# Attention with V as the held operand: two heads in the two halves of the array's columns, and probabilities divided ahead of their transposes

## The chip, the core and the metric

The kernel runs on one core of one Trainium2 chip. A core has five engines that run side by side, each with an instruction queue of its own: TensorE (PE in the profile; its weight loads are PEld), VectorE (DVE), ScalarE (ACT), GpSimd (POOL) and SyncE (SP, which here issues the loads from memory). The metric is the device time of one execution in microseconds (us); lower is better.

## The reference

A two-layer decoder trunk on 256 tokens of 1024 features, in float32. Layer 0 mixes tokens with a gated recurrence, layer 1 with attention; each layer has a SwiGLU feed-forward block of width 2816 before and after its mixer. The change lies in the attention of layer 1 (16 heads of 64, causal, with a forget gate whose running sum `c` is added to the logits):

```python
for blk in range(S // Q_BLOCK):            # two blocks of 128 queries
    q0 = blk * Q_BLOCK
    end = q0 + Q_BLOCK
    logits = jnp.einsum('bhqd,bhkd->bhqk', q[:, :, q0:end], k[:, :, :end]).astype(jnp.float32)
    logits = logits + c[:, :, q0:end, None] - c[:, :, None, :end]
    logits = jnp.where(kpos[None, :] <= qpos[:, None], logits, -jnp.inf)
    p = jax.nn.softmax(logits, axis=-1).astype(v.dtype)
    outs.append(jnp.einsum('bhqk,bhkd->bhqd', p, v[:, :, :end]))
o = jnp.concatenate(outs, axis=2).transpose(0, 2, 1, 3).reshape(Bn, S, D_ATTN)
return o @ w_o
```

## The kernel before

The 256 tokens are two tiles of 128 (t = 0 and 1). Every large product is made of three matmuls in a fast float32 form: operands are split into an upper and a lower part (`hi`, `lo`), and `mm3` (L183) adds hi x hi, hi x lo and lo x hi into one PSUM bank. Weights stream in from memory in tiles of 128 x 1024 (`load_raw`, issued by SP into five buffers) and are split by `split` (L165): ScalarE copies the upper part (L174), VectorE subtracts to get the lower part (L179). For the output projection `w_o` (`row_items` with `dve=True`) every second tile is split the other way: VectorE copies the upper part (L172), GpSimd subtracts (also L179).

TensorE's order is the program's own: it runs what the code issues, in that order. The other engines' orders are set by a scheduler when the program is built, with work inside `tc.high_priority()` put first; once built, each engine's order is fixed and each engine works through its queue strictly in turn.

In the attention stage the string `ATT_ORDER` (L1105) is TensorE's order: `0` and `1` are weight blocks of the projections for token tile 0 or 1 (first the query projection, sixteen entries in all, then the output projection), `a0` and `a1` are attention steps of a tile. A step works on head groups, of four heads for tile 0 (`per` = 4, one key tile) and of two heads for tile 1 (`per` = 2, two key tiles). Step i issues up to four things: the logits of group i (`logits`), the products with V of group i-3 (`values`), the transposes of the probabilities of group i-2 (`turn`), and, after every eighth head, the transposes of the output (`output`). Within `logits`, VectorE adds the mask (L1031) and takes the negative row maximum (L1033), and ScalarE takes the exponentials of each head into `pe` with the row sum as a side result in `sm` (L1038). `turn` makes four transposes of 128 x 128 into a PSUM bank (L1046), and ScalarE copies them to `pT` (L1048). `values` holds the transposed probabilities in the array and moves 64 columns of V (L1057), with the queries on the partitions of the result `po`; when eight heads are done, VectorE inverts the row sums (L1060) and multiplies (L1062) into `ot`. `output` transposes `ot` back to features on partitions (L1069), and writes its upper part on ScalarE (`oh`, L1072) and its lower part on VectorE (`ol`, L1073) as operands of the output projection.

While tile 0 is attended, the query projection of tile 1 (block by block) and its head transposes (`heads_T`, L921, L926, L929, L930) run between the steps.

Of the kernel before, what the change touches and what calls it, by code (L numbers as in the profile page):

```python
# [9 lines left out]
F32 = mybir.dt.float32  # L10
F32R = mybir.dt.float32r
BF16 = mybir.dt.bfloat16
AF = mybir.ActivationFunctionType
ALU = mybir.AluOpType
AX = mybir.AxisListType

P = 128
# [8 lines left out]
HD = 64  # L26
# [18 lines left out]
def trunk_kernel(ctx: ExitStack, tc: tile.TileContext, A: dict, out: bass.AP):  # L45
    nc = tc.nc
# [11 lines left out]
    def nm(s):  # L58
        uid[0] += 1
        return f"{s}_{uid[0]}"  # L60

    def mmbank():
        return psum.tile([P, 512], F32, tag="mm", name=nm("mm"), bufs=4)

    def gtbank():
        return psum.tile([P, 512], F32, tag="gt", name=nm("gt"), bufs=2)

    def trbank():
        return psum.tile([P, 512], F32, tag="tr", name=nm("tr"), bufs=2)
# [44 lines left out]
    ident = cpool.tile([P, P], F32, name="ident")  # L114
# [760 lines left out]
    kv = {}  # L875
# [133 lines left out]
    att = {}  # L1009
# [7 lines left out]
    def attention(t):  # L1017

        ap = pools["a"]
        nk = t + 1  # L1020
        per = 4 // nk
        mask = kv["cmask"].unsqueeze(1).to_broadcast([P, per, P])
        box = {}
        G = NH // per

        def logits(hg):
            hds = range(hg * per, (hg + 1) * per)
            ps = gtbank().rearrange("p (a b) -> p a b", a=per)
            for j, hd in enumerate(hds):
                nc.tensor.matmul(ps[:, j, :], att["q"][t][:, hd, :], kv["kT"][:, hd, :nk * P], start=True, stop=True)  # L1030
            nc.vector.tensor_tensor(ps[:, :, t * P:], ps[:, :, t * P:], mask, ALU.add)  # L1031
            mx = spool.tile([P, 4], F32, tag="mx", name=nm("mx"))
            nc.vector.tensor_reduce(mx[:, :per], ps, AX.X, ALU.max, negate=True)  # L1033
            if hds[0] % 8 == 0:
                box["sm"] = spool.tile([P, 8], F32, tag="sm", name=nm("sm"))
            pe = ap.tile([P, per, nk * P], F32, tag="pe", name=nm("pe"), bufs=3)
            for j, hd in enumerate(hds):
                nc.scalar.activation(pe[:, j, :], ps[:, j, :], AF.Exp, bias=mx[:, j:j + 1],  # L1038
                                     accum_out=box["sm"][:, hd % 8:hd % 8 + 1])
            box["pe", hg], box["s", hg] = pe, box["sm"]  # L1040

        def turn(hg):
            tp = trbank()
            pev = box["pe", hg].rearrange("p a b -> p (a b)")
            for j in range(4):
                nc.tensor.transpose(tp[:, j * P:(j + 1) * P], pev[:, j * P:(j + 1) * P], ident)  # L1046
            pT = box["pT", hg] = ap.tile([P, 4, P], F32, tag="pT", name=nm("pT"), bufs=3)
            nc.scalar.activation(pT.rearrange("p a b -> p (a b)"), tp, AF.Copy)  # L1048

        def values(hg):  # L1050
            hds = range(hg * per, (hg + 1) * per)
            if hds[0] % 8 == 0:
                box["po"] = mmbank()
            po, pT, sm = box["po"], box["pT", hg], box["s", hg]
            for j, hd in enumerate(hds):
                for k in range(nk):
                    nc.tensor.matmul(po[:, (hd % 8) * HD:(hd % 8 + 1) * HD], pT[:, j * nk + k, :],  # L1057
                                     kv["v"][k][:, hd * HD:(hd + 1) * HD], start=k == 0, stop=k == nk - 1)
            if hds[-1] % 8 == 7:
                nc.vector.reciprocal(sm, sm)  # L1060
                ot = box["ot", hds[-1] // 8] = ap.tile([P, 8, HD], F32, tag="ot", name=nm("ot"), bufs=2)
                nc.vector.tensor_tensor(ot, po.rearrange("p (a b) -> p a b", a=8),  # L1062
                                        sm.unsqueeze(2).to_broadcast([P, 8, HD]), ALU.mult)

        def output(b):
            otv = box["ot", b].rearrange("p a b -> p (a b)")
            tp = trbank()
            for j in range(4):
                nc.tensor.transpose(tp[:, j * P:(j + 1) * P], otv[:, j * P:(j + 1) * P], ident)  # L1069
            oh_v = att["oh"][t][:, 4 * b:4 * b + 4, :].rearrange("p a b -> p (a b)")  # L1070
            ol_v = att["ol"][t][:, 4 * b:4 * b + 4, :].rearrange("p a b -> p (a b)")
            nc.scalar.activation(oh_v, tp, AF.Copy)  # L1072
            nc.vector.tensor_tensor(ol_v, tp, oh_v.bitcast(F32), ALU.subtract)  # L1073

        steps = []
        for i in range(G + 4):
            s = []
            if i < G:
                s.append(lambda i=i: logits(i))
            if 0 <= i - 3 < G:  # L1080
                s.append(lambda i=i: values(i - 3))
            if 0 <= i - 2 < G:
                s.append(lambda i=i: turn(i - 2))
            j = i - 4
            if j >= 0 and (j + 1) * per % 8 == 0:
                s.append(lambda j=j: output((j + 1) * per // 8 - 1))
            steps.append(s)
        return steps

# [3 lines left out]
    for n in range(2):  # L1093
# [8 lines left out]
    ffn_items(lambda: pools["f"], A["ffn2_w_gate"][1], A["ffn2_w_up"][1], A["ffn2_w_down"][1], A["ffn2_post_g"][1],  # L1102
              lambda t: None, last=True)

    ATT_ORDER = ("0 0 0 0 0 0 0 0 a0 1 a0 1 1 1 a0 1 a0 1 a0 1 a0 a1 1 a0 "  # L1105
                 "0 a1 a0 a1 0 a1 0 a1 0 a1 0 a1 0 a1 0 a1 0 a1 1 a1 1 a1 1 1 1 1 1 1")


    def half(t, i):
# [161 lines left out]
    defer(6, att_rows)  # L1271

    steps = [attention(0), attention(1)]
    nxt = [n_ffn3, n_ffn3]
    for c in ATT_ORDER.split():
        if c[0] == "a":
# [46 lines left out]
```

## Time and profile before

| | |
|---|---|
| median of 3 runs | 1000.72 us (1000.6 to 1001.02) |
| the profiled execution | 1001.29 us |
| its span, first to last instruction | 999.3 us |
| granted TensorE clock, mean | 0.998 |
| attention stage | about 743 to 798 us of the span |

Row names in the views: a line number of the kernel, the engine, the operation, the tile written and the tiles read. In the list of groups the columns are count, total busy time and mean ns of one. In the view of stages each engine has its busy time and, in brackets, its instruction count, in the order PE, PEld, DVE, ACT, POOL; then come the granted clock, the DMA engines' share and GB/s. In the chain in order of time a row has the start, what the step added to the chain, and the step. In the timeline a row has the start and the duration of an instruction (or of a few of one kind, x4), and in square brackets how long its engine was idle before and what ended that. Matmuls overlap in the pipeline, so what a matmul costs is the step to the next one, not its own duration.

### The profile page before, as it was taken

How to read it: one execution, taken by the hardware profiler on the slowest of the kernel's cores; microseconds unless marked ns; L12 is line 12 of the kernel's file. 1: busy time of each engine (PE TensorE's matmuls, PEld its weight loads, DVE VectorE, ACT ScalarE, POOL GpSimd, SP SyncE). 2: the span in 40 equal slices, each digit the busy share in tenths (PEclk: the TensorE clock that was granted, in tenths of full speed). 3: DMA queues.
4: the chain of work that ended last, by engine and by line, in shares of the span. 5: the costliest groups of instructions: out<-in, count | busy, mean ns of one | idle time of the engine just before them, and what ended most of it. 6: DMA issues, size and time to landing. Idle time of an engine off the chain costs nothing.

```text
span 999.3 us, 12923 instructions
## 1 busy us (share of the span) xinstructions
PE 991.0 (99%) x4792; PEld 829.4 (83%) x4792; DVE 613.3 (61%) x775; ACT 533.1 (53%) x750; POOL 59.4 (6%) x97
## 2 busy tenths in 40 slices
PE   9999999999999999999999999999999999999997
PEld 6888888899988888888898888888888888888886
DVE  6756554668998555554786655554488475555542
ACT  7546444569986544443564444444466565444431
POOL 2400000100004000000100000000033000000000
PEclk9999999999999999999999999999999999999999
DMA  8967555565336766555467566555555066665531
GB/s 281 313 190 207 186 190 189 161 186 160 115 111 215 223 174 192 186 189 190 124 214 229 175 189 189 180 181 191 165 171 169 6 206 211 189 190 190 181 115 42
DMA packets 92644, 178.88 MB, mean 179 GB/s; under 512 B 11966, under 2 KB 32614, under 8 KB 92582
## 3 DMA queue, kind: packets, MB, share of 16 engines
q1 hardware_dynamic: 91142, 177.02, 55.9%
q10 hardware_dynamic: 608, 0.93, 0.3%
q8 instruction: 37, 0.61, 0.2%
q0 software_dynamic: 832, 0.12, 0.1%
q14 instruction: 25, 0.20, 0.1%
HBM read 176.95 MB, written 1.05 MB: 178 GB/s over the span
## 4 chain that ended last, share of the span: by engine, by line
PE 98%; DMA 1%; issue 1%; DVE 0%; ACT 0%; POOL 0%; DVEq 0%; POOLq 0%; ACTq 0%
PE mm L185 29%; PE mm L187 29%; PE mm L186 28%; PE tr L511 2%; PE gt L739 2%; PE gt L1030 1%; PE mm L192 1%; PE mm L194 1%; PE mm L1057 1%; PE mm L193 1%; PE mm L1171 1%; PE gt L216 1%; DMA raw<-in_ffn_w_gate_dram 1%; PE tr L1046 1%; PE tr L926 0%
## 5 line engine op out<-in xcount | busy, mean ns | idle before, releaser
L179 DVE TENSOR_TENSOR wlo<-raw,whi 128x1024 fp32r<-128x1024 f32 (+4 forms) x325 | 391.4, 1210 | 269.7 <-ACT whi L174 267.1
L174 ACT ACTIVATE whi<-raw 128x1024 fp32r<-128x1024 f32 (+4 forms) x325 | 337.7, 1045 | 315.3 <-PE mm L187 252.6
L185 PE MATMUL mm<-whi,xhi 128*128 128x512 f32 (+2 forms) x768 | 304.2, 396 | 0.0
L187 PE MATMUL mm<-whi,xlo 128*128 128x512 f32 (+2 forms) x768 | 298.8, 389 | 0.0
L186 PE MATMUL mm<-wlo,xhi 128*128 128x512 f32 (+2 forms) x768 | 298.0, 388 | 0.0
L187 PEld LDWEIGHTS mm<-whi,xlo 128*128 128x128 f32 x768 | 144.2, 188 | 30.4 <-DVE xlo L251 0.3
L186 PEld LDWEIGHTS mm<-wlo,xhi 128*128 128x128 f32 x768 | 144.5, 188 | 28.0 <-DVE wlo L179 0.3
L185 PEld LDWEIGHTS mm<-whi,xhi 128*128 128x128 f32 x768 | 144.3, 188 | 27.6
L185 PE MATMUL mm<-whi,hhi 128*128 128x512 f32 x352 | 138.6, 394 | 0.0
L187 PE MATMUL mm<-whi,hlo 128*128 128x512 f32 x352 | 137.9, 392 | 0.0
L186 PE MATMUL mm<-wlo,hhi 128*128 128x512 f32 x352 | 137.2, 390 | 0.0
L187 PEld LDWEIGHTS mm<-whi,hlo 128*128 128x128 f32 x352 | 66.1, 188 | 14.4
L186 PEld LDWEIGHTS mm<-wlo,hhi 128*128 128x128 f32 x352 | 66.1, 188 | 14.2
L185 PEld LDWEIGHTS mm<-whi,hhi 128*128 128x128 f32 x352 | 66.1, 188 | 13.5
L505 DVE SCALAR_TENSOR_TENSOR prod<-mm,rstd,sil 128x512 f32<-128x512 f32 (+1 forms) x48 | 33.9, 706 | 38.0 <-PE mm L187 34.3
L496 ACT ACTIVATE sil<-mm,rstd 128x512 f32<-128x512 f32 (+1 forms) x48 | 31.2, 652 | 40.5 <-PE mm L187 40.4
L200 POOL TENSOR_SCALAR nv<-ss 128x1 f32<-128x1 f32 x22 | 11.0, 502 | 702.6 <-ACT junk L207 702.6
L515 ACT ACTIVATE hhi<-tr 128x512 fp32r<-128x512 f32 (+1 forms) x48 | 26.6, 555 | 15.7 <-PE tr L511 15.6
L274 DVE TENSOR_TENSOR t<-mm,gb 128x512 f32<-128x512 f32 x24 | 16.2, 686 | 25.9 <-ACT junk L207 25.9
L516 DVE TENSOR_TENSOR hlo<-tr,hhi 128x512 fp32r<-128x512 f32 (+1 forms) x48 | 30.5, 643 | 1.4
L207 ACT ACTIVATE junk<-mm 128x512 bf16<-128x512 f32 x24 | 14.3, 597 | 31.7 <-PE mm L187 31.7
L185 PE MATMUL mm<-whi,zhi 128*128 128x340 f32 (+2 forms) x80 | 28.3, 354 | 0.0
(199 smaller groups left out, 936.1 us busy)
## 6 DMA issues: line engine op xcount, KB each, us to landing
raw<-in_ffn_w_down_dram SPq DMA_DIRECT2D x88, 512.0 KB
raw<-in_ffn_w_up_dram SPq DMA_DIRECT2D x80, 512.0 KB
raw<-in_ffn_w_gate_dram SPq DMA_DIRECT2D x78, 512.0 KB
raw<-in_rg_w_in_dram SPq DMA_DIRECT2D x20, 504.0 KB
raw<-in_rg_w_out_dram SPq DMA_DIRECT2D x10, 504.0 KB
raw<-in_ffn_w_gate_dram SPq DMA_DIRECT2D x18, 256.0 KB
raw<-in_ffn_w_up_dram SPq DMA_DIRECT2D x16, 256.0 KB
raw<-in_w_kv_dram SPq DMA_DIRECT2D x8, 512.0 KB
```

The costliest lines, as they stand in the source:

```text
L174: up = nc.scalar.activation(hi[:parts, c:c + m], rawv[:, c:c + m], AF.Copy)
L179: low.tensor_tensor(lo[:parts, c:c + m], rawv[:, c:c + m], hi[:parts, c:c + m].bitcast(F32), ALU.subtract)
L185: nc.tensor.matmul(ps, xh, wh, start=first, stop=False)
L186: nc.tensor.matmul(ps, xh, wl, start=False, stop=False)
L187: nc.tensor.matmul(ps, xl, wh, start=False, stop=last)
L274: nc.vector.tensor_tensor(t1[n], pf[n], gb[:, n * 512:(n + 1) * 512], ALU.mult)
L496: nc.scalar.activation(s[:, :nn], ps, AF.Silu, scale=rs[t][:, 0:1])
L505: nc.vector.scalar_tensor_tensor(pr[:, :nn], ps, rs[t][:, 0:1], s, ALU.mult, ALU.mult)
L511: nc.tensor.transpose(tp[:, j * P:(j + 1) * P], pr[:, j * P:(j + 1) * P], ident)
L515: nc.scalar.activation(hv, tp[:, :nn], AF.Copy)
L516: nc.vector.tensor_tensor(lv, tp[:, :nn], hv.bitcast(F32), ALU.subtract)
L739: nc.tensor.matmul(ps[:w, j * S:(j + 1) * S], wv[:, o:o + w], xc[:w, k, :], start=k == 0, stop=k == m - 1)
```

## The change

`values` now holds 64 columns of V of one head in the array and moves the transposed probabilities through it. The result has features on partitions. Two neighbouring heads write to partitions 0 to 63 and 64 to 127 of one bank, that is, they use the left and the right half of the array's columns. The result is already in the layout that the output projection needs, so `ot`, `output` and its transposes are gone; `oh` and `ol` are made straight from the bank of `values`. Since queries no longer lie on partitions there, the division by the row sums moves ahead: a new function `norm` inverts the sums of each group (L1044) and multiplies `pe` in place (L1045), one step after the logits and one step before the transposes (L1051, copied to `pT` at L1053; V products are at L1065, the upper and lower halves of the output at L1071 and L1072). There is one step less per token tile, and `ATT_ORDER` is adapted: tile 1's last query block comes before the last steps of tile 0, and there are two attention steps fewer in all.

```diff
-            box["pe", hg], box["s", hg] = pe, box["sm"]
+            box["pe", hg], box["s", hg] = pe, box["sm"][:, hds[0] % 8:hds[0] % 8 + per]
+
+        def norm(hg):
+            pe, sm = box["pe", hg], box["s", hg]
+            nc.vector.reciprocal(sm, sm)
+            nc.vector.tensor_tensor(pe, pe, sm.unsqueeze(2).to_broadcast([P, per, nk * P]), ALU.mult)
...
         def values(hg):
...
-            for j, hd in enumerate(hds):
+            for j in range(0, per, 2):
                 for k in range(nk):
-                    nc.tensor.matmul(po[:, (hd % 8) * HD:(hd % 8 + 1) * HD], pT[:, j * nk + k, :],
-                                     kv["v"][k][:, hd * HD:(hd + 1) * HD], start=k == 0, stop=k == nk - 1)
+                    for s in range(2):
+                        hd = hds[j + s]
+                        nc.tensor.matmul(po[s * HD:(s + 1) * HD, hd % 8 // 2, :], kv["v"][k][:, hd * HD:(hd + 1) * HD],
+                                         pT[:, (j + s) * nk + k, :], start=k == 0, stop=k == nk - 1)
             if hds[-1] % 8 == 7:
-                nc.vector.reciprocal(sm, sm)
-                ot = box["ot", hds[-1] // 8] = ap.tile([P, 8, HD], F32, tag="ot", name=nm("ot"), bufs=2)
-                nc.vector.tensor_tensor(ot, po.rearrange("p (a b) -> p a b", a=8),
-                                        sm.unsqueeze(2).to_broadcast([P, 8, HD]), ALU.mult)
-
-        def output(b):
-            otv = box["ot", b].rearrange("p a b -> p (a b)")
-            tp = trbank()
-            for j in range(4):
-                nc.tensor.transpose(tp[:, j * P:(j + 1) * P], otv[:, j * P:(j + 1) * P], ident)
-            oh_v = att["oh"][t][:, 4 * b:4 * b + 4, :].rearrange("p a b -> p (a b)")
-            ol_v = att["ol"][t][:, 4 * b:4 * b + 4, :].rearrange("p a b -> p (a b)")
-            nc.scalar.activation(oh_v, tp, AF.Copy)
-            nc.vector.tensor_tensor(ol_v, tp, oh_v.bitcast(F32), ALU.subtract)
+                b = hds[-1] // 8
+                oh_v = att["oh"][t][:, 4 * b:4 * b + 4, :].rearrange("p a b -> p (a b)")
+                ol_v = att["ol"][t][:, 4 * b:4 * b + 4, :].rearrange("p a b -> p (a b)")
+                nc.scalar.activation(oh_v, box["po"], AF.Copy)
+                nc.vector.tensor_tensor(ol_v, box["po"], oh_v.bitcast(F32), ALU.subtract)
...
-        for i in range(G + 4):
+        for i in range(G + 3):
             s = []
+            if 0 <= i - 1 < G:
+                s.append(lambda i=i: norm(i - 1))
...
-            j = i - 4
-            if j >= 0 and (j + 1) * per % 8 == 0:
-                s.append(lambda j=j: output((j + 1) * per // 8 - 1))
...
-    ATT_ORDER = ("0 0 0 0 0 0 0 0 a0 1 a0 1 1 1 a0 1 a0 1 a0 1 a0 a1 1 a0 "
-                 "0 a1 a0 a1 0 a1 0 a1 0 a1 0 a1 0 a1 0 a1 0 a1 1 a1 1 a1 1 1 1 1 1 1")
+    ATT_ORDER = ("0 0 0 0 0 0 0 0 a0 1 a0 1 1 1 a0 1 a0 1 1 a0 1 a0 a1 a0 "
+                 "0 a1 0 a1 0 a1 0 a1 0 a1 0 a1 0 a1 0 a1 1 a1 1 a1 1 1 1 1 1 1")
```

More of the change, by code (lines that the diff above doesn't have):

```diff
@@ L1053, in values @@
                 box["po"] = mmbank()
-            po, pT, sm = box["po"], box["pT", hg], box["s", hg]
-            for j, hd in enumerate(hds):
+            po, pT = box["po"].rearrange("p (a b) -> p a b", a=4), box["pT", hg]
+            for j in range(0, per, 2):
                 for k in range(nk):
-                    nc.tensor.matmul(po[:, (hd % 8) * HD:(hd % 8 + 1) * HD], pT[:, j * nk + k, :],
-                                     kv["v"][k][:, hd * HD:(hd + 1) * HD], start=k == 0, stop=k == nk - 1)
+                    for s in range(2):
+                        hd = hds[j + s]
+                        nc.tensor.matmul(po[s * HD:(s + 1) * HD, hd % 8 // 2, :], kv["v"][k][:, hd * HD:(hd + 1) * HD],
+                                         pT[:, (j + s) * nk + k, :], start=k == 0, stop=k == nk - 1)
             if hds[-1] % 8 == 7:
-                nc.vector.reciprocal(sm, sm)
-                ot = box["ot", hds[-1] // 8] = ap.tile([P, 8, HD], F32, tag="ot", name=nm("ot"), bufs=2)
-                nc.vector.tensor_tensor(ot, po.rearrange("p (a b) -> p a b", a=8),
-                                        sm.unsqueeze(2).to_broadcast([P, 8, HD]), ALU.mult)
-        def output(b):
-            otv = box["ot", b].rearrange("p a b -> p (a b)")
-            tp = trbank()
-            for j in range(4):
-                nc.tensor.transpose(tp[:, j * P:(j + 1) * P], otv[:, j * P:(j + 1) * P], ident)
-            oh_v = att["oh"][t][:, 4 * b:4 * b + 4, :].rearrange("p a b -> p (a b)")
-            ol_v = att["ol"][t][:, 4 * b:4 * b + 4, :].rearrange("p a b -> p (a b)")
-            nc.scalar.activation(oh_v, tp, AF.Copy)
-            nc.vector.tensor_tensor(ol_v, tp, oh_v.bitcast(F32), ALU.subtract)
+                b = hds[-1] // 8
[3 more added lines that the diff above has]
+                nc.vector.tensor_tensor(ol_v, box["po"], oh_v.bitcast(F32), ALU.subtract)
         steps = []
-        for i in range(G + 4):
+        for i in range(G + 3):
             s = []
+            if 0 <= i - 1 < G:
+                s.append(lambda i=i: norm(i - 1))
             if i < G:
```

## The prediction

> **What bounds the kernel now.** I read the page first (engine shares and the chain that ended last), then the busy time by stage, then the chain in order of time around the attention, then the timelines of the engines there.
>
> ```profile
> PE 991.0 (99%) x4792; PEld 829.4 (83%) x4792; DVE 613.3 (61%) x775; ACT 533.1 (53%) x750; POOL 59.4 (6%) x97
> PE 98%; DMA 1%; issue 1%; DVE 0%; ACT 0%; POOL 0%; DVEq 0%; POOLq 0%; ACTq 0%
> 743.00:762.00 19.00, 18.97 (x126) 16.85 (x125) 15.48 (x22) 11.49 (x40) 7.66 (x4) 1.00 0.45 139
> 762.00:785.00 23.00, 23.00 (x141) 20.38 (x140) 13.44 (x23) 11.89 (x34) 2.80 (x1) 1.00 0.20 69
> ```
>
> TensorE (PE) carries 98% of the chain, and in the attention stage (743 to 798 us) it is never idle (18.97 of 19.00 us, 23.00 of 23.00). So any matmul time that goes or comes counts in full, and a wait of PE is a loss in full. VectorE (DVE, the fourth figure) is the next engine: from 743 to 762 us, where token tile 0 is attended, it is busy for 15.48 of 19.00 us. Spare there: 3.5 us. Later (762 to 785) it has 9.6 us spare.
>
> **Removed from PE.** The chain in order of time prices each step of a head group, by what it adds to the chain:
>
> ```profile
> 754.63 0.84 PE mm L1057 x8
> 755.47 0.44 PE tr L1046 x4
> 797.10 0.44 PE tr L1069 x4
> 753.74 0.89 PE gt L1030 x8
> ```
>
> The four output transposes (L1069, one set per half of the heads and token tile) go: 4 x 0.44 = 1.75 us off the path. The logits (L1030) and the transposes of the probabilities (L1046) stay.
>
> **The value products.** Twelve groups at 0.84 us each (L1057; every f32 matmul shows as two passes, so eight passes of 0.105). Before, the probabilities are loaded (128 columns) and 64 columns of V move. After, 64 columns of V are loaded and 128 columns of probabilities move, still eight passes a group. A pass that moves 128 f32 columns costs 0.107 to 0.111 (0.89 / 8 in L1030's row), so eight one after the other are 0.86 us. The order of the passes is two of head A (left half of the columns), two of head B (right half), two of A, two of B. If B's first pass runs beside A's second, and so on, five pass times are on the path: 0.535 us. No row shows two halves at work at once; bounds are 0.43 (four pass times) and 0.86. I take 0.535, because two passes of one head must follow each other while its neighbour uses other columns.
>
> The Trainium skill, "TensorEngine Tiling (Array Packing)", sections Theoretical Speedup and Key Properties, puts two column tiles at up to 2x and says that they operate in parallel; that would be 0.42 us of body, and the whole sum below would come out at +2.0 us and not +2.95. No row of before can show it.
>
> The program narrows the stationary to 64 columns, and the trace has a nearest row for a switch to narrow columns: the cumulative sum, whose stationary has 16 columns.
>
> ```profile
> 522.83 0.15 PE mm L187
> 522.98 0.32 PE gt L959 x2
> 523.30 0.35 PE mm L185
> 523.66 0.16 PE mm L186
> 522.91 0.11 PEld L959 LDWEIGHTS gt<-triu,lf 128*16 128x16 f32 x2 [0.21 <-issue]
> 523.23 0.19 PEld L185 LDWEIGHTS mm<-whi,zhi 128*128 128x128 f32 x1 [0.21 <-issue]
> 795.65 0.29 PE mm L185
> ```
>
> The first four rows are the chain, the next two the weight loads: on both sides the load is held for 0.21 us, where elsewhere it runs under the matmul before. L959 and the matmul behind it took 0.32 + 0.35 = 0.67 us; two passes of 0.107 and an ordinary 0.16 with the 0.06 that a wide matmul loses after any group of passes (0.29 in the last row against the usual 0.23) make 0.43: the switch in and out cost 0.24 us. The first load, which now cannot be hidden, has 64 columns and not 16; at 0.105 us for 128 columns (a pass of L1057) that is 0.04 more: 0.28 us, in all twelve groups. Bounds: nothing, if the hold was due to that place, and 0.42 (both holds whole).
>
> So a group costs 0.535 + 0.28 = 0.815 us against 0.84: 12 x -0.025 = -0.3 us. The promise of the two halves is eaten by the two switches.
>
> **Added to VectorE, and the wait it makes.** New are twelve reciprocals and twelve multiplications (128x512, both operands in SBUF) ahead of the transposes; four reciprocals and four divisions of the output go. At a multiplication's 0.68 and a reciprocal's 0.19 (rows below) that is 8 x 0.87 = 7 us more, and it is now a step that PE waits for: exponentials, reciprocal, multiplication, transposes. For token tile 1 there is room: per group 0.43 mask, 0.69 maximum, 0.19 and 0.68 are 2.0 us in a PE cycle of 3.5. I find at most 0.2 us of wait, at the last but one group (the copy of its transposes queues behind two square sums on ScalarE). For token tile 0 there is none, and a lock makes it worse:
>
> ```profile
> L796 DVE TENSOR_TENSOR tt<-tt,xc 126x512 f32<-126x512 f32 x5 | 3.2, 681 | 0.0
> 746.39 2.39 POOL L179 TENSOR_TENSOR wlo<-raw,whi 128x1024 fp32r<-128x1024 f32 x1 [6.94 <-DVE whi L172]
> 747.24 0.69 DVE L1033 TENSOR_REDUCE mx<-gt 128x4 f32<-128x512 f32 x1
> 748.98 1.23 DVE L179 TENSOR_TENSOR wlo<-raw,whi 128x1024 fp32r<-128x1024 f32 x1 [1.05 <-ACT whi L174]
> 751.56 0.75 DVE L921 TENSOR_SCALAR htok<-mm,rstd 128x512 f32<-128x512 f32 x1
> 751.61 2.39 POOL L179 TENSOR_TENSOR wlo<-raw,whi 128x1024 fp32r<-128x1024 f32 x1 [2.83 <-DVE whi L172]
> 752.23 0.19 DVE L1060 RECIPROCAL sm<-sm 128x8 f32<-128x8 f32 x1
> 752.34 0.68 DVE L1031 TENSOR_TENSOR gt<-gt,cmask 128x512 f32<-128x512 f32 x1
> 752.92 2.16 DVE L179 TENSOR_TENSOR wlo<-raw,whi 128x1024 fp32r<-128x1024 f32 x1
> 755.61 0.68 DVE L172 CAST whi<-raw 128x1024 fp32r<-128x1024 f32 x1
> 756.36 2.38 POOL L179 TENSOR_TENSOR wlo<-raw,whi 128x1024 fp32r<-128x1024 f32 x1 [2.36 <-DVE whi L172]
> 759.63 0.69 DVE L930 COPY qT<-tr 64x512 f32<-64x512 f32 x1
> ```
>
> Each odd row block of the output weights is split by a cast on DVE (L172) and a subtraction on GpSimd (POOL, 2.39 us) that starts as the cast ends. While it ran (751.61 to 754.00), DVE's own subtraction of two SBUF operands took 2.16 us and not 1.23: it ended 1.1 us after POOL did. The mask (PSUM) beside it kept its 0.68. So a DVE operation with two SBUF operands is held until POOL is through, and the new multiplication is one. In DVE's order in the changed program, one multiplication stands one to four places behind each of the four casts.
>
> The walk along that order (a step after a PSUM operand takes some 0.65 from start to start, a subtraction 1.2; the first 747.9 us are as before). Multiplication 0 is held by the first POOL subtraction to 748.8: harmless. Then subtraction, copy, cast to 751.9, reciprocal, token scaling (L921); POOL holds 751.95 to 754.35; multiplication 1 ends at 755.0. Then mask, subtraction, maximum, mask, cast to 758.65, maximum, reciprocal at 759.4; POOL holds to 761.05; multiplication 2 ends at 761.75. Then subtraction, copy, cast to 764.2; reciprocal, low half of the first output (L1072 after), scaling to 765.7; POOL holds to 766.7; multiplication 3 ends at 767.4.
>
> What PE would want:
>
> ```profile
> 754.47 1.00 PE L1057 MATMUL mm<-v,pT 128*128 128x64 f32 x8
> 755.67 0.47 PE L185 MATMUL mm<-whi,xhi 128*128 128x512 f32 x1
> 757.14 0.60 PE L926 MATMUL tr<-ident,htok 128*128 128x128 f32 x4
> 755.72 0.37 ACT L1038 ACTIVATE pe<-gt,mx 128x128 f32<-128x128 f32 x1 [2.72 <-DVE mx L1033]
> 757.10 0.61 ACT L1048 ACTIVATE pT<-tr 128x512 f32<-128x512 f32 x1
> 760.05 1.06 ACT L174 ACTIVATE whi<-raw 128x1024 fp32r<-128x1024 f32 x1
> ```
>
> Values 0 at 754.47 and 0.82 long, transposes 1 at 755.3, then (the new order has one projection block more here) block 1.44, transposes of the queries 0.44, block 1.44, values 1 at 759.05, transposes 2 at 759.9, block 1.44, values 2 at 761.8, transposes 3 at 762.6. They get multiplication 1 in time, 2 at 761.75 and 3 at 767.4. ScalarE's chain (four exponentials 755.72 to 757.10, copy 0.61, upper half 1.06) adds some 0.4 us at values 1, inside that wait. PE is idle for 767.4 - 762.6 = 4.8 us, longest piece about 2.9. Behind it in PE's queue wait the logits of token tile 1, so all later work is late by as much, and DVE and ScalarE regain their lead. The queue that issues the loads (SP) waits for the delayed subtractions too; loads of later weights are issued later, but the DMA engines have room in this stage (share 0.20 above). The end of the stage is neutral: after the last values the same two blocks and eight transposes pass before the low half of the output is needed.
>
> **Sum.** -1.75 - 0.3 + 4.8 + 0.2 = +2.95 us on the profiled 1001.29 us: 1004.2. That execution is 0.57 above the median of the runs shown, 1000.72, so the median goes to 1003.7.
>
> **Rivals.** (1) The halves don't overlap, so the change saves nothing on the array: a group is 0.86 + 0.28 = 1.14 us, 12 x 0.30 = +3.6, of which 0.9 (three groups) vanishes in the wait before transposes 3: -1.75 + 3.6 + 3.9 + 0.2 = +5.95, median 1006.7. For it: every pass of the trace follows the one before by at least 0.105 us. Chance 0.15.
>
> (2) Not slower: the port does not hold the multiplications. Then DVE needs only its own time: multiplication 2 ends at 758.5, 3 at 763.4, PE waits 0.85 us, and the sum is -1.75 - 0.3 + 0.85 + 0.2 = -1.0, median 999.7. It decides at the casts: if POOL's subtraction starts after the multiplication, or the multiplication runs beside it, the wait is gone. For it: the held row is a single one, and the mask and reciprocal were not held; against: it has two SBUF operands just like the held one. Chance 0.18. By the rule in the Trainium skill, "SBUF — State Buffer", on the shared port pair (an exclusive lock that a DVE operation with two SBUF inputs shares with GpSimd, the loser blocked for the whole instruction), this rival falls; 2.16 us agrees with the rule.
>
> (3) The switch is free: a group is 0.535 us, -3.7 in all, but PE reaches transposes 3 earlier and waits 5.6: -1.75 - 3.7 + 5.6 + 0.2 = +0.4, median 1001.1. Chance 0.12.
>
> (4) Both (2) and (3): -1.75 - 3.7 + 1.7 + 0.2 = -3.5, median 997.2. Chance 0.10.
>
> **Numbers.** The forecast has 0.45. A measurement of this kernel tells 0.2% (2 us) from no change. The forecast gives 0.40 slower and 0.05 same (the bounds of the body and the switch); (1) 0.15 slower; (2) 0.14 same, 0.04 faster; (3) 0.09 same, 0.03 slower; (4) 0.10 faster. Together 0.14 faster, 0.28 same, 0.58 slower. The range reaches from (2), with some room, to (1): 999.3 to 1007.0; it leaves out (4) and a little at each end.
>
> **What would show it.** Right: no L1069 work; a value group of about 0.8 us with both switches in it, the weight load held on either side; PE idle ahead of the third and fourth transposes of token tile 0, released by DVE's multiplication; multiplications of more than 1.5 us where POOL's subtraction runs. Wrong: multiplications of 0.68 there, value groups of 0.55 or of 1.1 us, or PE busy throughout from 755 to 768 us.

## The result and the profile after

The changed kernel takes 1005.12 us (median of 8 runs, 1002.11 to 1005.47) against 1000.87 us before (8 runs, 1000.44 to 1002.11): a ratio of 1.0038, with a 95% interval of 1.0027 to 1.0048. It is slower, by 4.25 us. The profiled execution took 1005.15 us; its span is 1003.4 us and its mean granted clock 0.996.

The page's engine line and its chain line:

```profile
PE 991.3 (99%) x4776; PEld 823.4 (82%) x4776; DVE 622.7 (62%) x791; ACT 532.7 (53%) x750; POOL 58.4 (6%) x97
PE 95%; DVE 2%; issue 1%; DMA 1%; ACT 0%; POOL 0%; DVEq 0%; ACTq 0%; POOLq 0%
```

The two stretches of the attention stage in the view of stages:

```profile
743.00:762.00 19.00, 17.35 (x112) 14.43 (x111) 18.44 (x23) 11.41 (x41) 7.16 (x3) 1.00 0.41 114
762.00:785.00 23.00, 20.16 (x106) 15.38 (x105) 15.36 (x28) 9.14 (x25) 2.35 (x1) 0.85 0.30 90
```

TensorE has 16 matmuls less (the 4 x 4 output transposes), yet its busy time is the same; its share of the chain fell from 98% to 95%. In the first stretch VectorE (fourth figure) is busy for 18.44 of 19.00 us, and TensorE, never idle before, lacks 1.65 us there and 2.84 us in the next stretch. That next stretch shows something the prediction has no term for: the granted clock is 0.85 and not 1.00.

What TensorE waited for in this stage (total us, times, longest):

```profile
PE tr L1051 <- DVE pe L1045: 4.5, 2, 2.8
```

The timelines of VectorE's multiplications, of GpSimd, and of TensorE's transposes behind the waits:

```profile
752.09 2.23 DVE L1045 TENSOR_TENSOR pe<-pe,sm 128x512 f32<-128x512 f32 x1
758.57 2.33 DVE L1045 TENSOR_TENSOR pe<-pe,sm 128x512 f32<-128x512 f32 x1
764.74 1.59 DVE L1045 TENSOR_TENSOR pe<-pe,sm 128x512 f32<-128x512 f32 x1
751.38 2.39 POOL L179 TENSOR_TENSOR wlo<-raw,whi 128x1024 fp32r<-128x1024 f32 x1 [3.08 <-DVE sm L1044]
757.98 2.37 POOL L179 TENSOR_TENSOR wlo<-raw,whi 128x1024 fp32r<-128x1024 f32 x1 [4.21 <-PE tr L926]
763.44 2.35 POOL L179 TENSOR_TENSOR wlo<-raw,whi 128x1024 fp32r<-128x1024 f32 x1 [3.09 <-DVE sm L1044]
761.05 0.63 PE L1051 MATMUL tr<-ident,pe 128*128 128x128 f32 x4 [1.65 <-DVE pe L1045]
766.48 1.03 PE L1051 MATMUL tr<-ident,pe 128*128 128x128 f32 x4 [2.84 <-DVE pe L1045]
```

Each multiplication overlaps a GpSimd subtraction and ends some 0.55 us after it: GpSimd ends at 753.77, 760.35 and 765.79 us, the multiplications at 754.32, 760.90 and 766.33. Two of the three are late for TensorE. The second wait brings the clock down, as shorter windows of the view of stages show (ahead of PEclk stand the five engines):

```profile
765.00:766.40 1.40, 0.00 (x0) 0.00 (x0) 1.40 (x2) 0.00 (x0) 0.78 (x1) 1.00 0.50 193
768.00:770.00 2.00, 2.00 (x11) 1.12 (x10) 0.72 (x2) 0.20 (x1) 0.00 (x0) 0.50 0.85 231
772.00:773.00 1.00, 1.00 (x4) 0.75 (x3) 0.71 (x2) 0.00 (x0) 0.00 (x0) 0.50 0.00 0
774.00:776.00 2.00, 2.00 (x12) 1.67 (x11) 1.12 (x2) 0.51 (x2) 0.00 (x0) 1.00 0.00 0
```

So TensorE runs at half clock from its restart at 766.5 to between 773 and 774 us. In the chain in order of time the same steps cost double there, and are back to normal in the value group of tile 1 that follows:

```profile
767.50 1.71 PE gt L1030 x4
769.21 1.05 PE mm L1065 x8
771.41 0.43 PE mm L187
773.12 1.06 PE gt L1030 x4
776.87 0.44 PE tr L1051 x4
778.69 0.86 PE gt L1030 x4
779.55 0.59 PE mm L1065 x8
780.14 0.59 PE tr L1051 x4
```

At full clock a value group adds 0.59 us and the transposes behind it 0.59 us, 1.18 together, where the kernel before had 0.84 + 0.44 = 1.28. An ordinary set of transposes is still 0.44 (776.87, behind logits and not behind a value group), so 0.15 of its 0.59 is the switch out of narrow columns, and by the same token 0.15 of the value group's 0.59 the switch in; the eight passes themselves take 0.44. That split is worked out here; two experiments test it.

### The profile page after: what moved, and what is told of

Same layout as the page of the kernel before. It is cut to its first block, busy times and chain, and to the rows that moved or that the text cites. A ratio compares the mean times of both kernels' runs of the same rounds, so it can differ in the third digit from the quotient of the medians.

```text
span 1003.4 us, 12912 instructions
## 1 busy us (share of the span) xinstructions
PE 991.3 (99%) x4776; PEld 823.4 (82%) x4776; DVE 622.7 (62%) x791; ACT 532.7 (53%) x750; POOL 58.4 (6%) x97
## 4 chain that ended last, share of the span: by engine, by line
PE 95%; DVE 2%; issue 1%; DMA 1%; ACT 0%; POOL 0%; DVEq 0%; ACTq 0%; POOLq 0%
PE mm L185 28%; PE mm L187 28%; PE mm L186 28%; PE tr L511 2%; PE gt L739 2%; PE mm L192 1%; PE mm L194 1%; PE mm L193 1%; PE gt L1030 1%; PE mm L1169 1%; PE gt L216 1%; DMA raw<-in_ffn_w_gate_dram 1%; PE mm L1065 1%; PE tr L1051 1%; DVE pe L1045 1%
```

## The experiments

Theory A: the change is a gain on the array, which the division loses again: GpSimd's subtractions hold the multiplications, TensorE waits 4.5 us for them, and its clock halves after the longer wait. Rivals: the narrow value products cost more than they save; the division costs by VectorE's own load, without GpSimd; the clock dips for another reason. The expectations, each written ahead of its run, call some versions by short names: e2 is the one without GpSimd's subtractions, e6 the one with pairs of groups, e7 the one with the early output block.

**Without the division.** Function `norm` is emptied; the probabilities stay undivided.

```diff
-            pe, sm = box["pe", hg], box["s", hg]
-            nc.vector.reciprocal(sm, sm)
-            nc.vector.tensor_tensor(pe, pe, sm.unsqueeze(2).to_broadcast([P, per, nk * P]), ALU.mult)
+            pass
```

> The changed kernel without the reciprocals and the multiplications on VectorE (L1044, L1045): the probabilities are left undivided. Theory A (the loss is PE's wait for held multiplications of token tile 0, and the halved clock behind that wait; on the array itself the change gains 1.75 us of transposes and about 0.1 us in each of twelve value groups): no wait ahead of the transposes, clock 1.00 in the stage, 997 to 998.5 us. Rival B (the two switches in each value group are the loss, the wait only shows it): 1002 us or more. Rival C (the other order of steps is the loss): 1002 us or more.

Measured: 997.51 us (997.05 to 997.81), ratio 0.9968, interval 0.9955 to 0.998. The trace has no wait of TensorE in the stage. So the rest of the change gains 3.4 us against before (997.51 against 1000.87), and the division costs 7.6 us (1005.12 - 997.51), which is more than the 4.5 us of waiting.

**Without GpSimd's subtractions.** The output weights are split as all other weights are.

```diff
-              lambda t, accs: enter(t, [main_dest(GI[("ffn2", 1)], t)], accs, gbox["mix1"], False), dve=True, rows0=1)
+              lambda t, accs: enter(t, [main_dest(GI[("ffn2", 1)], t)], accs, gbox["mix1"], False), rows0=1)
```

> The changed kernel with all output weights split on ScalarE and VectorE, none on GpSimd (dve=False in row_items of w_o). VectorE gets four subtractions of 1.2 us for four casts of 0.6 us, 2.4 us more in all. Theory A with the port as the cause: each multiplication takes 0.69 us, PE waits under 1 us in all, the clock stays at 1.00, 998 to 999.5 us. Rival D (VectorE simply has too much work for token tile 0, the port adds little): PE waits at least as long as in the changed kernel, 1004 us or more.

Measured: 998.99 us, ratio 0.9985 (0.9977 to 0.9994). TensorE's wait in the stage:

```profile
PE tr L1051 <- DVE pe L1045: 1.5, 1, 1.5
```

Two multiplications of token tile 0 in VectorE's timeline:

```profile
757.18 0.68 DVE L1045 TENSOR_TENSOR pe<-pe,sm 128x512 f32<-128x512 f32 x1
762.48 0.69 DVE L1045 TENSOR_TENSOR pe<-pe,sm 128x512 f32<-128x512 f32 x1
```

The same multiplication takes 0.68 us and not 2.3, with the same operands and more other work on VectorE: the hold is GpSimd's. The waits are 3.0 us shorter (1.5 against 4.5), and the clock stays at 1.00 in the stage; with the 3.1 us that the half clock costs (measured below) that makes the 6.1 us between the two versions. VectorE's own load leaves one wait of 1.5 us, where below 1 was expected.

**The control for that: the kernel before without GpSimd's subtractions.** The same edit in the kernel before.

> The kernel before with only the GpSimd subtractions of the output weights taken out (as in the other versions without them), a control. In the kernel before TensorE is never idle in the attention stage, so the split by GpSimd costs it nothing there: if so, this is 1000.9, within 0.1% of before, and the whole gain of the versions without GpSimd belongs to the changed attention. If the GpSimd split itself costs the kernel before something (or saves it), this kernel shows it: below 1000 (or above 1002) then, and the gain has to be shared out.

Measured: 1001.91 us (1001.68 to 1002.59), ratio 1.0012 (1.0002 to 1.0021). So GpSimd's help is worth 1.2 us to the kernel before. ScalarE has more copies without it, and TensorE now waits for exponentials:

```profile
PE tr L1046 <- ACT pe L1038: 0.7, 2, 0.4
```

0.7 of the 1.2 us is this wait; the other 0.5 I have not placed. With equal splits, the change is a gain of 2.9 us (998.99 against 1001.91).

**The waits filled.** Seven and twelve matmuls on constants, into a bank that is overwritten, stand ahead of the transposes of groups 2 and 3 of token tile 0. They use up the waiting time, so that the array stays busy while VectorE is as late as before.

```diff
+            for _ in range((0, 0, 7, 12)[hg] if t == 0 else 0):
+                nc.tensor.matmul(tp, nc.const_aps.tensor(1.0, (P, P), BF16), nc.const_aps.tensor(1.0, (P, 512), BF16),
+                                 start=True, stop=True)
```

> The changed kernel with idle matmuls (constants, 128x512) put into PE's queue ahead of the transposes of groups 2 (seven) and 3 (twelve) of token tile 0, into the bank that the transposes then overwrite. They fill the waits and change nothing else. Theory A with the clock as a separate term: the transposes start when they did (multiplications 2 and 3 end no sooner), but the clock stays at 1.00 and the half-speed stretch of about 7 us is gone: some 3 us less than the changed kernel, 1001.5 to 1002.5 us. Rival E (the slow stretch behind the wait has another cause, such as the switch of columns): 1005 us as before.

Measured: 1002.42 us, ratio 1.0017 (1.0008 to 1.0026). In the view of stages of this kernel:

```profile
770.00:785.00 15.00, 15.00 (x93) 11.82 (x91) 10.15 (x22) 6.94 (x25) 0.00 (x0) 1.00 0.09 32
```

And in its chain:

```profile
766.73 0.66 PE tr L1054 x4
767.38 0.86 PE gt L1030 x4
768.25 0.59 PE mm L1068 x8
770.43 0.87 PE gt L1030 x4
```

The transposes of group 3 (L1054 here) start at 766.73 us, no earlier than in the changed kernel (766.48), but the clock is 1.00 and the steps are whole again. From these transposes to the end of the second group of logits behind them the same work takes 4.57 us here (770.43 + 0.87 = 771.30) and 7.70 in the changed kernel (773.12 + 1.06 = 774.18): 3.1 us is what the half clock costs in the profiled execution, 2.7 us between the medians (1005.12 - 1002.42). It is a term of its own beside the wait.

**One wait filled.** Only group 2's seven matmuls, so that a single idle stretch remains.

```diff
-            for _ in range((0, 0, 7, 12)[hg] if t == 0 else 0):
+            for _ in range((0, 0, 7, 0)[hg] if t == 0 else 0):
```

> The changed kernel with constant matmuls in the first of its two idle stretches alone (seven ahead of the transposes of group 2, none ahead of group 3's), so that TensorE is idle once, for about 2.8 us, rather than twice (1.65 and 2.84 us). If one idle stretch of 2.8 us is enough to halve the granted clock, the profile shows a clock near 0.5 from 766 to 773 us again and the median stays near 1005. If it takes the sum of both idle stretches, the clock stays at 1.00 and the median is near 1002.4, as with both filled.

Measured: 1005.43 us (1003.93 to 1006.55), ratio 1.0047 (1.0034 to 1.0059). Its one wait:

```profile
PE tr L1054 <- DVE pe L1045: 2.9, 1, 2.9
```

Two of its windows:

```profile
762.00:766.00 4.00, 2.25 (x17) 1.47 (x15) 3.94 (x6) 2.13 (x5) 1.91 (x1) 1.00 0.83 235
768.00:770.00 2.00, 2.00 (x8) 1.17 (x8) 0.81 (x2) 0.60 (x1) 0.00 (x0) 0.50 0.80 243
```

One idle stretch of 2.9 us is enough to halve the clock. Here it falls inside that stretch: the granted clock reads 0.50 from 766.36 us on, and TensorE restarts at 767.14. Filling the first wait alone brings nothing else either, since the second is set by VectorE.

**The division alone.** The kernel before, with probabilities divided ahead of their transposes, V moving as before, and the output copied where it was divided.

```diff
+        def norm(hg):
+            pe, sm = box["pe", hg], box["s", hg]
+            nc.vector.reciprocal(sm, sm)
+            nc.vector.tensor_tensor(pe, pe, sm.unsqueeze(2).to_broadcast([P, per, nk * P]), ALU.mult)
...
-                nc.vector.reciprocal(sm, sm)
...
-                nc.vector.tensor_tensor(ot, po.rearrange("p (a b) -> p a b", a=8),
-                                        sm.unsqueeze(2).to_broadcast([P, 8, HD]), ALU.mult)
+                nc.vector.tensor_copy(ot, po.rearrange("p (a b) -> p a b", a=8))
```

> The kernel before with the division alone moved ahead of the transposes: per-group reciprocal and multiplication, the output copied instead of divided; value products, output transposes and the order of steps as before. Theory A: PE waits 3 to 5 us for the multiplications of token tile 0, and the clock falls if one wait is near 3 us: 1004 to 1009 us. Rival B or C: within 1 us of before, 1000 to 1002 us.

Measured: 1009.19 us, ratio 1.0086 (1.0073 to 1.01), just above the expected stretch. TensorE's waits:

```profile
PE tr L1051 <- DVE pe L1045: 4.4, 2, 3.2
PE mm L1062 <- ACT pT L1053: 1.2, 1, 1.2
```

The windows behind them:

```profile
760.00:770.00 10.00, 5.63 (x30) 5.02 (x30) 7.18 (x8) 3.52 (x12) 2.93 (x2) 0.84 0.52 157
770.00:785.00 15.00, 15.00 (x79) 12.73 (x77) 10.81 (x21) 7.18 (x21) 0.00 (x0) 0.88 0.12 35
```

The loss of 8.3 us comes with the division alone: 5.6 us of waits, and the low clock behind a wait of 3.2 us. So the narrow products are not its cause.

**All passes of one half, then of the other.** This and the following ones have no subtraction on GpSimd, and are compared with 998.99 us. The order of the eight passes of a group is changed.

```diff
-            for j in range(0, per, 2):
-                for k in range(nk):
-                    for s in range(2):
+            for s in range(2):
+                for j in range(0, per, 2):
+                    for k in range(nk):
```

> The version without GpSimd splits (e2), with the value products of a group in another order: first all passes of the heads in the left half of the columns, then all of the right half. Same products, same switches. Theory G (the two halves work at once, a half takes 0.107 us for a pass of 128 columns): the eight passes take about 0.75 us in place of 0.44, 0.3 us more in each of twelve groups, of which some 0.9 falls into the wait ahead of the transposes of group 3: 1001.5 to 1002.6 us. Rival F (a pass is short because only 64 columns are loaded, the halves don't matter): 999 us, as e2.

Measured: 999.08 us, ratio 0.9981 (0.9973 to 0.999), and in the chain:

```profile
780.16 0.59 PE mm L1065 x8
780.75 0.59 PE tr L1051 x4
```

Unchanged, so of these two orders of the passes neither is better. This left two readings of 0.44 us: two halves at work at once, or a pass that is short because it loads only 64 columns.

**All passes in the left half.** The same order, but the right half's heads are computed in the left half too, and the left half's result is copied to both places.

```diff
-                        nc.tensor.matmul(po[s * HD:(s + 1) * HD, hd % 8 // 2, :], kv["v"][k][:, hd * HD:(hd + 1) * HD],
+                        nc.tensor.matmul(po[:HD, hd % 8 // 2, :], kv["v"][k][:, hd * HD:(hd + 1) * HD],
...
```

> The version without GpSimd's subtractions, in which all eight passes of a value group are put into the left half of the columns (the right half's four heads are computed into the left one too and the left half is copied to both places of the result; so the result of the right half is left out). If eight passes last 0.44 us because the two halves of the columns work at once, eight passes in one half can't overlap: the group shows about 0.86 to 1.0 us in the chain in place of 0.59, and the run is about 12 x 0.4 = 5 us longer than the version with both halves (998.9), so near 1003.9. If a pass is short because it needs 64 columns of weights only, whatever half they lie in, the group stays at 0.59 and the time at 999.

Measured: 1003.29 us (one run), and in the chain:

```profile
774.07 1.02 PE mm L1065 x8
775.09 0.59 PE tr L1051 x4
```

TensorE's wait in the stage:

```profile
PE tr L1051 <- DVE pe L1045: 0.5, 1, 0.5
```

Now the group is 1.02 us: less the 0.15 of the switch, 0.87 in place of 0.44. The two halves do work at once, and in a group of eight passes they overlap completely (0.87 / 0.44 = 2.0). Twelve groups make 5.2 us; the wait of 1.5 us shrank to 0.5 meanwhile, and 4.2 of the 4.3 us are explained.

**Two groups per narrow stretch.** Token tile 1's values are issued for two groups together, so that four switches in and out go.

```diff
-            if 0 <= i - 3 < G:
-                s.append(lambda i=i: values(i - 3))
+            if 0 <= i - 3 < G and (t == 0 or i % 2 == 0):
+                for g in ((i - 3,) if t == 0 else (i - 4, i - 3)):
+                    s.append(lambda g=g: values(g))
```

> The version without GpSimd splits (e2), with the value products of token tile 1 issued for two groups at a time, in every second step: four narrow stretches in place of eight. Theory H (each stretch pays about 0.3 us for the switch in and out): 4 x 0.3 = 1.2 us less than e2, 997.8 us. Rival (the switch is free, or hidden): as e2, 999 us.

Measured: 999.82 us (998.46 to 1000.95), ratio 0.9988 (0.9979 to 0.9997): the gain did not come. The chain of the profiled run (998.46 us):

```profile
775.61 1.02 PE mm L1065 x16
776.63 0.58 PE tr L1051 x4
779.47 0.44 PE tr L1051 x4
```

TensorE's waits in it:

```profile
PE tr L1051 <- DVE pe L1045: 2.5, 2, 1.5
```

The switch is priced right: a pair costs 1.02 + 0.58 + 0.44 = 2.04 us, two single groups 4 x 0.59 = 2.36, so one switch in and out is 0.32. What took the gain in the profiled run is a new wait of 1.0 us ahead of the last group's transposes. VectorE's timeline shows where it comes from:

```profile
789.90 0.16 DVE L1044 RECIPROCAL sm<-sm 128x2 f32<-128x2 f32 x1
790.34 0.75 DVE L286 SCALAR_TENSOR_TENSOR h<-t,rstd,h 128x512 f32<-128x512 f32 x1 [0.29 <-POOL rstd L202]
791.01 0.69 DVE L1045 TENSOR_TENSOR pe<-pe,sm 128x512 f32<-128x512 f32 x1
```

In this version's order VectorE has a step of the layer's output (L286) between the last group's reciprocal and its multiplication, and that step waits for GpSimd. In e2 the multiplication follows its reciprocal at once (790.49 and 790.68 us). Had it done so here, it would have ended near 790.8 us by this estimate, and TensorE was ready for it at 790.86: the wait comes from VectorE's order, which the scheduler made anew for this version. The median is a further 1.1 us above what the two terms give (998.99 - 1.28 + 1.0 = 998.7): six of the eleven runs took 999.82 us or more, none of them is the profiled one, and why is open.

**An output block moved ahead of the late transposes**, without pairs (e7): one `0` of `ATT_ORDER` goes before the step that transposes group 3 of token tile 0, to cover the 1.5 us.

```diff
-    ATT_ORDER = ("0 0 0 0 0 0 0 0 a0 1 a0 1 1 1 a0 1 a0 1 1 a0 1 a0 a1 a0 "
-                 "0 a1 0 a1 0 a1 0 a1 0 a1 0 a1 0 a1 0 a1 1 a1 1 a1 1 1 1 1 1 1")
+    ATT_ORDER = ("0 0 0 0 0 0 0 0 a0 1 a0 1 1 1 a0 1 a0 1 1 a0 1 0 a0 a1 a0 "
+                 "a1 0 a1 0 a1 0 a1 0 a1 0 a1 0 a1 0 a1 1 a1 1 a1 1 1 1 1 1 1")
```

> The version without GpSimd splits (e2), with one block of the output projection of token tile 0 moved ahead of the step that transposes group 3 of tile 0, where e2 still waits 1.5 us. Theory A: useful work fills the wait, 1 to 1.5 us less than e2, 997.5 to 998 us. Rival: the wait moves to the next step that VectorE feeds (the first transposes of tile 1), as e2, 999 us.

Measured: 998.08 us (997.77 to 998.26), ratio 0.9969 (0.9956 to 0.9981). The only wait left is this:

```profile
PE gt L1030 <- ACT pe L1038: 0.2, 1, 0.2
```

That is 0.9 us less than e2, a little short of the 1 to 1.5 us expected.

**Both of the last two.**

> e6 and e7 together on e2. If both gains stand by themselves: 2.2 to 2.7 us less than e2, 996.3 to 996.8 us, below both the kernel before and the changed kernel. If they draw on the same wait: 997.5 to 998 us.

Measured: 997.9 us (997.84 to 998.4), ratio 0.9969 (0.9956 to 0.9981). The 1.0 us wait of the pairs is still there, and with it the 1.2 us that they save are nearly gone: the two gains don't add up.

**Pairs that leave the last group alone.** The early block, and token tile 1's values in five stretches (one group, three pairs, one group), so that work stays ahead of the last transposes.

```diff
-            if 0 <= i - 3 < G:
-                s.append(lambda i=i: values(i - 3))
+            if t == 0 or i in (3, G + 2):
+                vals = [i - 3] if 0 <= i - 3 < G else []
+            else:
+                vals = [i - 4, i - 3] if 3 < i < G + 2 and i % 2 == 1 else []
+            for g in vals:
+                s.append(lambda g=g: values(g))
```

> The version with the early output block, in which token tile 1's values are done in five narrow stretches (one group, three pairs, one group) rather than eight, with the last group's transposes still covered by other work. If each stretch costs a switch in and out of about 0.31 us, three fewer save 0.9 us: near 997.2 against 998.08, with pairs of 1.02 us in the chain and no wait of the transposes on VectorE's multiplications of 1 us. If the work kept in the order does not cover the last groups, a wait of the transposes near 1 us comes back and the time stays at 998.

Measured: 997.29 us (996.89 to 998.0), ratio 0.9964 (0.9951 to 0.9978). In its chain a pair reads:

```profile
784.95 1.02 PE mm L1065 x16
785.98 0.59 PE tr L1051 x4
```

The pairs are there at their price, and the only wait of TensorE in the stage is 0.2 us for exponentials, as with the early block alone. VectorE's last multiplication follows its reciprocal at once again (788.94 and 789.12 us). This is the fastest version: 3.6 us ahead of the kernel before by its ratio, 4.6 us ahead of the kernel before with the same splits. Against the early block alone it is 0.8 us by medians, near the expected 0.9, but the ranges overlap (997.77 to 998.26 there) and the two were not run together.

## Why the prediction came out as it did

The direction and the main mechanism were right, and 1005.12 us lies within the range. Step by step:

- **Output transposes.** Gone, as said (-1.75 us).
- **Value group.** Forecast 0.815 us against 0.84, measured 0.74 with both switches: -0.10 a group, -1.2 us in all and not -0.3. The mis-sized term is the body. The step "two passes of one head must follow each other while its neighbour uses other columns" gave five pass times; the chain shows four (0.44 us). The switch, taken from the 16-column rows of the cumulative sum at 0.28 us, measured 0.30 to 0.32, so that term was right. On the body the Trainium skill, "TensorEngine Tiling (Array Packing)", Theoretical Speedup and Key Properties, was nearer: up to 2x and tiles that operate in parallel, against 2.0 measured here. Key Properties also says that a change of tiling mode drains the array, which agrees with a switch that costs. (By the prediction's own terms the 0.42 us body that it names would have given +1.9 us, not +2.0: 12 x 0.115 less, of which three groups' 0.345 return in the wait.)
- **The hold.** The walk along VectorE's order put the ends of multiplications 1 to 3 at 755.0, 761.75 and 767.4 us; they came at 754.3, 760.9 and 766.3. The waits were put at 4.8 us, the longest near 2.9; they were 4.5 and 2.84. This agreement is partly luck: VectorE finished earlier than the walk had it, and TensorE was ready earlier too (at 759.40 and 763.64 us, where the prediction has 759.9 and, with the first wait, 764.45), so the two errors cancel in the waits. That the hold is GpSimd's was argued from one row (2.16 us); the version without GpSimd shows it.
- **Token tile 1.** The 0.2 us of wait did not come: the list of TensorE's waits has the two of tile 0 only.
- **Missed: the clock.** The step "all later work is late by as much" was wrong. The work behind the wait is also slower: 3.1 us in the profiled execution. I had looked at the granted clock of before, 1.00 in both stretches shown, and did not ask what an idle stretch of 2.9 us does to it.

The account: the division costs 4.5 us of waiting and 3.1 us of clock, together the 7.6 us that taking it out gave back. (Between medians it splits as 4.9 and 2.7: the version with filled waits is 4.9 us above the one without the division.) The rest of the change gains 1.75 + 1.2 = 2.95 us by its terms, and 3.4 by the version without the division; 0.4 us of gain has no place yet. The traces put about half of it in the stage: from the first logits to the first transposes behind the attention (L216) it takes 55.63 us before (743.14 to 798.77) and 52.46 without the division (742.92 to 795.38), 3.2 us less and not 2.95. So the forecast of +2.95 us was 1.3 us short: the clock is +3.1, the body, the wait, tile 1 and the unplaced gain are -0.9, -0.3, -0.2 and -0.4. That the measured time lies so near the forecast is in part luck, since a missed term of 3.1 us and a mis-sized one of 0.9 work against each other.

Of the rivals, the one where the port does not hold is refuted. Its 999.7 us is near the kernel without GpSimd's subtractions (998.99), but not for its reasons: it had 0.85 us of wait and 0.3 us from the value groups, where 1.5 and 1.2 were measured. That the halves don't overlap is refuted by the left-half version, whose 1.02 us is what that rival would have looked like. What the prediction says for that rival, that every pass follows the one before by at least 0.105 us, holds within a running group only: the shortest step between two matmul records of before is 0.025 us (L511). A free switch is refuted by the pairs.

## What to carry to other kernels

When a step moves into the path of the bounding engine, price it with what its engine shares with others, not with its duration alone: multiplications of 0.68 us, two of which came late, cost 7.6 us here. A wait of the bounding engine of a few us can have a second price in the clock afterwards, so cover it with any useful work, as the early output block does. Use narrow column halves in long stretches, and look in the new trace at what the changed order did to the other engines' queues: a step put ahead of the multiplication took back what the pairs had saved.

## What the runs showed of the hardware

- **The clock halves after a short idle stretch.** In three traces TensorE's clock went from 1.00 to 0.50 in an idle stretch of 2.89 us (one wait filled) or 3.17 us (the division alone), or 0.1 us behind one of 2.84 us (the changed kernel). With one wait filled it fell after only 2.1 us of idling (764.25 to 766.35 us). Stretches of 1.65 us (the first wait of the changed kernel) and of 1.52 and less (in other traces) brought no fall. Half speed lasted 6.8 us each time (766.56 to 773.38 us in the changed kernel). The Trainium skill, "TensorE: Matmul & The Clock Gate", in its first part on the clock gate, puts the fall at an idle window of about 3.4 us and the recovery at about as long a busy one. Here the fall came with less and the recovery took about twice that; the measurement decides.
- **The clock changes on a grid.** In the traces' records of the clock the first stretch at full speed is 986.45, 989.87, 993.28 or 996.69 us long in the runs without a fall in the stage: multiples of 3.413 us, from 289 to 292. Half speed lasted two such steps (6.83 us). The grid lies differently from run to run, so what an idle stretch does should depend also on where it falls on the grid. One run in eight of the changed kernel took 1002.11 us with a mean clock of 0.998, as the version with filled waits does; I take it that it escaped the fall, which such a grid allows, but that run was not traced. The version with a single wait of 1.5 us had eight runs from 998.51 to 999.36 us and three from 1000.27 to 1001.14. Whether the clock is behind these is open: none of the three was traced, and the kernel before, without any such wait, has runs of 1002.01 to 1002.08 us beside a median of 1000.88.
- **A VectorE step with two operands in SBUF is held while GpSimd works.** The multiplication took 0.68 us alone, and 2.23 and 2.33 beside a GpSimd subtraction of 2.4 us, ending 0.55 us after it.
- **The two column halves overlap fully**, in both orders of the passes that were run (0.44 us for eight passes of 128 f32 columns, 0.87 in one half).
- **A switch in and out of narrow columns costs 0.30 to 0.32 us**, half on each side. The half paid on the way out is 0.15 us behind 8 passes and behind 16.
